# A decoder layer: the second MLP matrix as Strassen block products, with its running result and the sums of weight blocks in HBM

## Chip, cores and metric

The kernel runs on one core of a Trainium2 chip. The metric is the device time of one execution in microseconds (us). The kernel before takes 1024.85 us, the median of three runs (1024.71 to 1026.03).

## The reference

One decoder layer over 576 tokens: a prompt of 512 and 8 samples of 8 tokens. The width is 1024, the MLP is 4096 wide, all in 32-bit floats.

```
h = rmsnorm(x); z = h @ w_in                       # 1024 -> 6912
retention, window attention and short convolution  # "the mixer"
mixed = sum_n sigmoid(gate_n) * (branch_n @ w_branch_n) @ w_out
x = x + rmsnorm(mixed)
f = square(relu(rmsnorm(x) @ w_ff1)) @ w_ff2       # 1024 -> 4096 -> 1024
x = x + rmsnorm(f)
x = x + sigmoid(rmsnorm(x) @ w_ple_gate) * (p @ w_ple_proj)
```

## The kernel before

Activations lie feature by feature: 8 blocks of 128 features on the partitions, 576 tokens along a row, worked in two halves of 288. Every product is done with three matmuls, because both factors are split into a high part (rounded to the format that TensorE reads, `fp32r`) and a low part: high x high, high x low, low x high.

All weights lie in one tensor `W` of panels, in the order of use. A panel is 128 x 1024 (512 KB): mostly the 8 blocks that make one output column of 128 features. `prep` (L140 to L142) loads a panel on SP's queue into `wst` (2 buffers), ScalarE casts the high part `whi`, VectorE subtracts to get the low part `wlo` (3 buffers each); `nextw` prepares two panels ahead. `unit` (with `mm`, L324) does one panel: 8 blocks x 3 matmuls x 2 halves = 48 matmuls into two PSUM banks `pm`. `stats` and `rsqrt` make the norms: a matmul, VectorE, a power on GpSimd (L378), VectorE again.

The order on each engine is a scheduler's: it walks the instructions by priority and puts each on its engine's queue when its model has the inputs and a free buffer. An engine then works through its queue in order. SP only issues DMAs.

The program has the mixer (from the start to about 496 us), the output projection with the first norm, and the MLP in four quarters c of 1024 hidden features. A quarter is eight columns of the first matrix (f1) and then eight panels of the second (f2), whose result is added into a tile `f` in SBUF (L983). For c = 0, f1 and f2 are plain units. For c = 1 to 3, f1 is done in pairs of columns (m, m+4) by a Strassen (Winograd) scheme: the 8 x 2 blocks of a pair's weights and the two halves of the tokens make a 2 x 2 problem, with 7 block products of 12 matmuls in place of 8 (`pairs`, `product`, L216). The sums of operand blocks (`xs`) are made once, for the norm's output. The four sums of weight blocks of a pair, t3, t2, t1 and t4, are made on VectorE (`Pair.prep`, L182, L188, L192, L197) just before the split into high and low parts (L162, L163). After each product the `done_a` function takes relu and square (L1020 to L1029). f2 is plain units in every quarter.

At the end of the MLP stand `handover` (second norm and the start of the last gate) and eight gate panels with the output.

Of the kernel before, what the change touches and what calls it, by code (L numbers as in the profile page):

```python
# [1 line left out]

# [27 lines left out]
def panels():  # L30

    out = []
# [23 lines left out]
    out.append([("pp", k, m) for m in range(4) for k in range(2)])  # L56
    for c in range(4):
        if c == 0:
            cols("f1", range(8))
        else:  # L60
            for m in range(8 * c, 8 * c + 4):
                cols("f1", [m + 4, m])
        out.extend([[("f2", 8 * c + k, m) for k in range(8)] for m in range(8)])
    out.append([("pp", k, m) for m in range(4, 8) for k in range(2)])
    cols("pg", range(8))
    return out
# [3 lines left out]
def decoder_step(ctx: ExitStack, tc: tile.TileContext, xT, pT, W, consts, smalls, s0q, s0t, ckT, cv,  # L70
# [49 lines left out]
    plan = panels()  # L120
# [26 lines left out]
    def wtile():  # L147
        ph, pl = wpools[nprep[0] % len(wpools)]
        nprep[0] += 1
        return (ph.tile([P, 8, P], F32R, tag="whi", name=nm("whi")), pl.tile([P, 8, P], F32R, tag="wlo", name=nm("wlo")))  # L150
# [9 lines left out]
    def whalves(raw, n=8):  # L160
        hi, lo = wtile()
        A.copy(out=hi[:, :n, :], in_=raw[:, :n, :])  # L162
        V.tensor_tensor(out=lo[:, :n, :], in0=raw[:, :n, :], in1=hi[:, :n, :].bitcast(F32), op=ALU.subtract)  # L163
        return hi, lo
# [4 lines left out]
    class Pair:  # L169
# [7 lines left out]
        def prep(self, j):  # L177
            Q = 4 * P
            a, c = rawtile(), rawtile()
            load(c, W[j])  # L180
            load(a[:, :4, :], W[j + 1][:, :Q])
            V.tensor_tensor(out=a[:, 4:, :], in0=c[:, :4, :], in1=c[:, 4:, :], op=ALU.add)  # L182
            g = whalves(a)
            self.w["b11"], self.w["t3"] = (g, 0), (g, 4)
            yield
            b = rawtile()
            load(b[:, 4:, :], W[j + 1][:, Q:])
            V.tensor_tensor(out=b[:, :4, :], in0=a[:, :4, :], in1=a[:, 4:, :], op=ALU.add)  # L188
            g = whalves(b)
            self.w["t2"], self.w["b21"] = (g, 0), (g, 4)  # L190
            yield
            V.tensor_tensor(out=c[:, :4, :], in0=c[:, :4, :], in1=a[:, :4, :], op=ALU.add)  # L192
            g = whalves(c)
            self.w["t1"], self.w["b22"] = (g, 0), (g, 4)
            yield
            d = rawtile()
            V.tensor_tensor(out=d[:, :4, :], in0=b[:, :4, :], in1=b[:, 4:, :], op=ALU.add)  # L197
            self.w["t4"] = (whalves(d, 4), 0)
            yield
# [18 lines left out]

    class Operands:


        def __init__(self, xh, xl):
            self.xh, self.xl = xh, xl
            self.s = []

        def make(self, src, j):

            xa, xb = tmpt(), tmpt()
            src(j, xa)
            src(j + 4, xb)  # L230
            t = stmp.tile([P, 4, H], F32, tag="stmp", name=nm("stmp"))
            V.tensor_tensor(out=t[:, 0, :], in0=xb[:, HS[1]], in1=xa[:, HS[1]], op=ALU.subtract)
            V.tensor_tensor(out=t[:, 1, :], in0=xa[:, HS[0]], in1=t[:, 0, :], op=ALU.subtract)
            V.tensor_tensor(out=t[:, 2, :], in0=xa[:, HS[0]], in1=xa[:, HS[1]], op=ALU.add)
            V.tensor_tensor(out=t[:, 3, :], in0=xb[:, HS[0]], in1=t[:, 1, :], op=ALU.subtract)
# [3 lines left out]
            split(t, hi, lo)  # L239
            self.s.append((hi, lo))  # L240

        def __call__(self, name):
            if name in ("a11", "a12", "a22"):
                k0, h = 4 * (name[2] == "2"), HS[name[1] == "2"]
                return lambda j: (self.xh(k0 + j)[:, h], self.xl(k0 + j)[:, h])
            i = ("s1", "s2", "s3", "x3").index(name)
            return lambda j: (self.s[j][0][:, i, :], self.s[j][1][:, i, :])
# [4 lines left out]
    def pairs(js, X, make, done, ahead):  # L252
# [3 lines left out]
        prev = None  # L256
        for i, j in list(enumerate(js)) + [(None, None)]:
            q = None
            if i is not None:
                while len(groups) < i + 1 or "t1" not in groups[i].w:  # L260
                    next(make)
                q = Job()
                q.w, q.n = groups[i].w, i
                q.a, q.e, q.b = bank("pa"), bank("pe"), bank("pbb")
                product(q.a, q.w["b11"], X("a11"), True)
                A.activation(q.b[:, :H], q.a[:, :H], AF.Copy, scale=-1.0)
                product(q.e, q.w["t3"], X("s3"), True)
                q.es = halft()
                A.copy(out=q.es, in_=q.e[:, :H])
                next(make, None)  # L270
            if prev is not None:
                product(prev.e, prev.w["t4"], X("a22"), False)
                done(prev, "c21")
            if q is not None:
                product(q.b, q.w["t2"], X("s2"), False)
                A.copy(out=q.e[:, :H], in_=q.b[:, :H])
                next(make, None)
                product(q.a, q.w["b21"], X("a12"), False)
                done(q, "c11")
            if prev is not None:  # L280
                product(prev.b, prev.w["b22"], X("x3"), False)
                done(prev, "c12")
# [4 lines left out]
            elif ahead:  # L287
                ahead()
# [907 lines left out]
```

## Time and profile before

| | |
|---|---|
| median of three runs | 1024.85 us |
| the profiled execution | 1025.21 us |
| its span | 1023.4 us |
| TensorE busy, granted clock | 99%, 0.998 of full speed |
| VectorE, ScalarE, GpSimd busy | 59%, 37%, 5% |
| HBM read, written | 91.33 MB, 8.29 MB |

The span is the time from the first to the last instruction that the profiler saw; 1.8 us lie around it. Busy times count an engine's instructions once where they overlap. In the groups of instructions a mean is that of one instruction by itself; matmuls overlap, so means of theirs add up to more than the time that passed. A DMA share is the mean busy share of the core's 16 DMA engines.

### The profile page before, as it was taken

How to read it: one execution, taken by the hardware profiler on the slowest of the kernel's cores; microseconds unless marked ns; L12 is line 12 of the kernel's file. 1: busy time of each engine (PE TensorE's matmuls, PEld its weight loads, DVE VectorE, ACT ScalarE, POOL GpSimd, SP SyncE). 2: the span in 40 equal slices, each digit the busy share in tenths (PEclk: the TensorE clock that was granted, in tenths of full speed). 3: DMA queues.
4: the chain of work that ended last, by engine and by line, in shares of the span. 5: the costliest groups of instructions: out<-in, count | busy, mean ns of one | idle time of the engine just before them, and what ended most of it. 6: DMA issues, size and time to landing. Idle time of an engine off the chain costs nothing.

```text
span 1023.4 us, 17804 instructions
## 1 busy us (share of the span) xinstructions
PE 1009.6 (99%) x7477; PEld 977.8 (96%) x7477; DVE 603.0 (59%) x1119; ACT 383.5 (37%) x656; POOL 46.1 (5%) x49
## 2 busy tenths in 40 slices
PE   9999999999999999999999999999999999999998
PEld 8999999999999888899999999999999999999988
DVE  7534755543536766355528886267447744863886
ACT  7122322221213534233436544256225512653641
POOL 1100111000110000000001100000000000000110
PEclk9999999999999999999999999999999999999999
DMA  7321211222362211225413522123212511551122
GB/s 257 102 84 68 83 61 66 88 93 94 102 212 63 62 47 58 83 84 175 147 62 109 176 83 83 42 83 124 94 42 73 178 49 62 175 203 53 62 80 76
DMA packets 32112, 100.77 MB, mean 98 GB/s; under 512 B 3784, under 2 KB 6888, under 8 KB 31136
## 3 DMA queue, kind: packets, MB, share of 16 engines
q1 hardware_dynamic: 30672, 93.63, 28.3%
q0 software_dynamic: 1216, 5.94, 1.5%
q8 instruction: 58, 0.95, 0.4%
q14 instruction: 22, 0.18, 0.1%
q10 hardware_dynamic: 144, 0.06, 0.0%
HBM read 91.33 MB, written 8.29 MB: 97 GB/s over the span
## 4 chain that ended last, share of the span: by engine, by line
PE 84%; DVE 10%; DMA 2%; ACT 1%; issue 1%; POOL 1%; SPq 0%; POOLq 0%; DVEq 0%; ACTq 0%
PE pm L324 68%; PE pbb L216 4%; PE pa L216 3%; PE pe L216 3%; DMA wst<-in_W 1%; PE pb L732 1%; DVE wlo L142 1%; POOL rs_b L378 1%; DVE xl L402 1%; DVE hlf L907 1%; DVE x L908 1%; PE pb L713 1%; DVE fl L998 1%; PE pb L739 1%; DVE wlo L163 1%
## 5 line engine op out<-in xcount | busy, mean ns | idle before, releaser
L324 PE MATMUL pm<-xh,whi 128*128 128x288 f32 x1120 | 257.2, 301 | 0.8 <-ACT xh L401 0.4
L141 ACT CAST whi<-wst 128x1024 fp32r<-128x1024 f32 (+1 forms) x130 | 130.9, 1008 | 329.3 <-PE pm L324 253.9
L324 PE MATMUL pm<-xl,whi 128*128 128x288 f32 x1120 | 252.0, 296 | 2.1 <-DVE xl L402 2.0
L324 PE MATMUL pm<-xh,wlo 128*128 128x288 f32 x1120 | 251.6, 296 | 2.1 <-DVE wlo L142 2.1
L324 PEld LDWEIGHTS pm<-xh,whi 128*128 128x128 f32 x1120 | 183.7, 189 | 13.6 <-issue 8.4
L324 PEld LDWEIGHTS pm<-xl,whi 128*128 128x128 f32 x1120 | 183.8, 188 | 4.3 <-DVE xl L402 3.1
L324 PEld LDWEIGHTS pm<-xh,wlo 128*128 128x128 f32 x1120 | 183.9, 188 | 2.6 <-DVE wlo L142 2.6
L142 DVE TENSOR_TENSOR wlo<-wst,whi 128x1024 fp32r<-128x1024 f32 (+1 forms) x130 | 152.2, 1172 | 36.5 <-ACT whi L141 33.1
L324 PE MATMUL pm<-fl,whi 128*128 128x288 f32 x512 | 115.7, 298 | 1.9 <-DVE fl L998 1.9
L324 PE MATMUL pm<-fh,whi 128*128 128x288 f32 x512 | 115.9, 298 | 0.1
L324 PE MATMUL pm<-fh,wlo 128*128 128x288 f32 x512 | 115.5, 297 | 0.0
L410 DVE TENSOR_TENSOR tmp<-pm,rb 128x288 f32<-128x288 f32 x80 | 33.3, 451 | 97.2 <-PE pm L324 97.2
L324 PEld LDWEIGHTS pm<-fl,whi 128*128 128x128 f32 x512 | 84.6, 190 | 2.2 <-DVE fl L998 2.2
L324 PEld LDWEIGHTS pm<-fh,whi 128*128 128x128 f32 x512 | 84.6, 190 | 0.4 <-ACT fh L996 0.3
L324 PEld LDWEIGHTS pm<-fh,wlo 128*128 128x128 f32 x512 | 84.7, 190 | 0.0
L162 ACT CAST whi<-wst 128x1024 fp32r<-128x1024 f32 (+1 forms) x48 | 44.6, 942 | 95.3 <-PE pm L324 59.2
L378 POOL TENSOR_TENSOR rs_b<-rs_a,mhalf 128x9 f32<-128x9 f32 (+2 forms) x15 | 33.2, 2212 | 773.0 <-DVE rs_a L377 773.0
L163 DVE TENSOR_TENSOR wlo<-wst,whi 128x1024 fp32r<-128x1024 f32 (+1 forms) x48 | 51.8, 1089 | 26.7 <-ACT whi L162 25.1
L216 PE MATMUL pbb<-xs,whi 128*128 128x288 f32 x288 | 58.2, 295 | 0.0
L983 DVE TENSOR_TENSOR f<-f,pm 128x288 f32<-128x288 f32 x48 | 19.9, 450 | 47.9 <-PE pm L324 47.9
L216 PEld LDWEIGHTS pbb<-xs,whi 128*128 128x128 f32 x288 | 46.2, 188 | 0.0
L216 PE MATMUL pbb<-xs,wlo 128*128 128x288 f32 x144 | 42.5, 295 | 0.0
(248 smaller groups left out, 1478.4 us busy)
## 6 DMA issues: line engine op xcount, KB each, us to landing
wst<-in_W SPq DMA_DIRECT2D x134, 512.0 KB, 3.5
wst<-in_W SPq DMA_DIRECT2D x24, 256.0 KB, 2.6
x<-in_xT SPq DMA_DIRECT2D x10, 288.0 KB, 4.8
dx<-x POOLq DMA_DIRECT2D x2, 1152.0 KB, 4.6
x<-dx SPq DMA_DIRECT2D x2, 1152.0 KB, 7.2
out_yT<-x SPq DMA_DIRECT2D x16, 144.0 KB, 1.8
x<-in_xT SPq DMA_DIRECT2D x3, 576.0 KB, 6.6
tmp<-in_pT SPq DMA_DIRECT2D x4, 288.0 KB, 4.0
```

Source lines behind the costliest of these rows:

```text
L141: A.copy(out=hi[:, c, :], in_=st[:, c, :])
L142: V.tensor_tensor(out=lo[:, c, :], in0=st[:, c, :], in1=hi[:, c, :].bitcast(F32), op=ALU.subtract)
L162: A.copy(out=hi[:, :n, :], in_=raw[:, :n, :])
L163: V.tensor_tensor(out=lo[:, :n, :], in0=raw[:, :n, :], in1=hi[:, :n, :].bitcast(F32), op=ALU.subtract)
L216: PE.matmul(bank[:, :H], lhsT=lhs[:, s + j, :], rhs=rhs, start=start and j == 0 and i == 0, stop=j == 3 and i == 2, skip_group_check=True)
L324: PE.matmul(p[:, :H], lhsT=lhs[:, kw, :], rhs=rhs[:, HS[i]], start=s, stop=e)
L378: G.tensor_tensor(out=b, in0=a, in1=mhalf[:, :nb], op=ALU.pow)
L402: V.scalar_tensor_tensor(lo, src, gain(gi, k), hi.bitcast(F32), op0=ALU.mult, op1=ALU.subtract)
L410: V.tensor_tensor(out=out[:, HS[i]], in0=ps[i][:, :H], in1=r[:, HS[i]], op=ALU.mult)
L713: PE.matmul(p[g][:, i * w:i * w + w], lhsT=aq[grow(g), t + i, 128 * n:128 * n + 128], rhs=ak[grow(g), k0:k0 + w], start=True, stop=True)
L732: PE.matmul(po[grow(g), :], lhsT=avt[:, 128 * chunk + 64 * g:128 * chunk + 64 * g + 64], rhs=sb, start=kh == 0, stop=kh == nk - 1)
L983: V.tensor_tensor(out=fm, in0=fm, in1=ps[i][:, :H], op=ALU.add)
```

## The change

For c = 1 and 2 all eight columns of f2, and for c = 3 four of them, are done as pairs by the same scheme: pairs (m, m+4), for c = 3 (m, m+2). The square of the relu is stored in four quarter tiles `fq`, high and low halves together, and `Operands.make` builds the operand sums for f2 from the relu's results inside f1's pairs. Products of the last pair of f1 are finished by `rest` in front of f2's first pair, and that pair takes its products in another order.

The running result of f2 is no longer in SBUF. For c = 0 it is stored to eight HBM tensors `df` by SP; for c = 1 and 2 GpSimd adds to them by accumulating DMAs; for c = 3 they are loaded into `f`.

The four weight sums of all 22 pairs (12 of f1, 10 of f2) are built in HBM. A generator, `weight_sums`, has six stretches (five of 4 pairs, one of 2), two at a time, each in six steps; `nextw` calls for one step. A full stretch has DMAs of 1 MB: plain copies on SP, accumulating ones on GpSimd. `Pair.prep` then only loads pieces and splits them. The pools for split weights are smaller (one extra buffer for two, and two half buffers for t4).

```diff
+    def weight_sums():
+        def steps(j0, n):
+            t3, t2, t1, t4 = [spill.tile([P, n, Q], F32, name=nm("ts")) for _ in range(4)]
...
+            for t in (t3, t1):
+                nc.sync.dma_start(out=t, in_=block(0, 0))
+            yield
+            G.dma_start(out=t3, in_=block(0, 1), accum_op=ALU.add)
+            G.dma_start(out=t1, in_=block(1, 0), accum_op=ALU.add)
+            yield
+            nc.sync.dma_start(out=t2, in_=t3)
+            yield
+            G.dma_start(out=t2, in_=block(1, 0), accum_op=ALU.add)
+            yield
+            nc.sync.dma_start(out=t4, in_=t2)
+            yield
+            G.dma_start(out=t4, in_=block(1, 1), accum_op=ALU.add)
+            yield
+        for a in range(0, len(stretches), 2):
+            gens = [steps(*q) for q in stretches[a:a + 2]]
+            for _ in range(6):
+                for g in gens:
+                    next(g)
+                    yield
...
     def nextw(ahead=2):
+        next(wsums, None)
         j = pos[0]
...
-            V.tensor_tensor(out=a[:, 4:, :], in0=c[:, :4, :], in1=c[:, 4:, :], op=ALU.add)
-            g = whalves(a)
...
+            t3, t2, t1, t4 = sums[j]
+            for parts in ((("b11", W[j + 1][:, :Q]), ("t3", t3)), (("t2", t2), ("b21", W[j + 1][:, Q:])),
+                          (("t1", t1), ("b22", W[j][:, Q:])), (("t4", t4),)):
+                n = 4 * len(parts)
+                raw = rawtile()
+                hi, lo = wtile(n)
+                for i, (name, src) in enumerate(parts):
+                    load(raw[:, 4 * i:4 * i + 4, :], src)
+                    self.w[name] = (hi, lo), 4 * i
+                A.copy(out=hi, in_=raw[:, :n, :])
+                V.tensor_tensor(out=lo, in0=raw[:, :n, :], in1=hi.bitcast(F32), op=ALU.subtract)
+                yield
...
+    def rest():
+        q = last.pop()
+        product(q.b, q.w["b22"], q.X("x3"), False)
+        q.done(q, "c12")
+        product(q.e, q.w["t4"], q.X("a22"), False)
+        q.done(q, "c21")
...
+    def done_f(c, n):
+        def done(q, which):
...
+            if which in ("c21", "c12"):
+                G.dma_start(out=df[m], in_=q.t[m2], accum_op=ALU.add)
...
+    for c in range(1, 4):
+        Fc = Quads()
+        F[:] = [Fc, ((1, 0),) if c < 3 else (), Operands(Fc.at)]
+        pairs(4, ops, done_a)
+        n = 4 if c < 3 else 2
+        fops = F[2]
+        if c == 3:
+            rest()
+            f, X1, pps[0] = Act8(F32, "f"), Act8(F32, "x1"), bigt(F32, "pp")
+            for k in range(8):
+                nc.sync.dma_start(out=f(k), in_=df[k])
...
+        pairs(n, fops, done_f(c, n), True)
+    rest()
```

In what follows, `wst` are panels on their way in, `cst` the constants, `ts` the HBM tensors of the sums (of the first stretch: ts30 is t3, ts31 t2, ts32 t1, ts33 t4; of the second: ts58, ts59, ts60, ts61). SP's queue near the start, before:

```order
L449 DMA cst_112<-in_consts 128x2118
L140 DMA wst30_304<-in_W 128x1024
L140 DMA wst33_310<-in_W 128x1024
L140 DMA wst54_406<-in_W 128x1024
L140 DMA wst59_464<-in_W 128x1024
L140 DMA wst64_522<-in_W 128x1024
L140 DMA wst69_580<-in_W 128x1024
```

And of the change, from the same place (units 3 to 8 of the weights):

```order
L187 DMA ts30_304<-in_W 512x1x512
L187 DMA ts32_306<-in_W 512x1x512
L149 DMA wst34_310<-in_W 128x1024
L149 DMA wst37_316<-in_W 128x1024
L517 DMA cst_112<-in_consts 128x2118
L187 DMA ts58_412<-in_W 512x1x512
L187 DMA ts60_414<-in_W 512x1x512
L149 DMA wst62_418<-in_W 128x1024
L149 DMA wst67_478<-in_W 128x1024
L192 DMA ts31_305<-ts30_304 16x16384
L192 DMA ts59_413<-ts58_412 16x16384
L149 DMA wst72_538<-in_W 128x1024
```

Four copies of 1 MB have come ahead of the weights of unit 5, and two copies that need finished accumulates ahead of those of unit 7. Later on SP's queue, units 17 to 21 before:

```order
L140 DMA wst141_1177<-in_W 128x1024
L140 DMA wst156_1259<-in_W 128x1024
L140 DMA wst169_1349<-in_W 128x1024
L140 DMA wst176_1420<-in_W 128x1024
L140 DMA wst186_1492<-in_W 128x1024
```

And of the change, units 17 to 20 (ts280 to ts283 belong to the fifth stretch, ts295 to ts298 to the sixth):

```order
L149 DMA wst157_1213<-in_W 128x1024
L187 DMA ts295_2174<-in_W 256x1x512
L187 DMA ts297_2176<-in_W 256x1x512
L192 DMA ts281_2071<-ts280_2070 16x16384
L149 DMA wst172_1297<-in_W 128x1024
L192 DMA ts296_2175<-ts295_2174 16x8192
L149 DMA wst185_1389<-in_W 128x1024
L196 DMA ts283_2073<-ts281_2071 16x16384
L196 DMA ts298_2177<-ts296_2175 16x8192
L149 DMA wst192_1461<-in_W 128x1024
```

The last of all 24 copies stands directly ahead of the weights of unit 20; after it SP's queue holds no copy of sums any more. GpSimd's queue near the start, before (`rs_b` is the power of the first norm's two halves):

```order
L461 MEMSET rq50_395 128x2304
L378 ISA
L378 TENSOR_TENSOR rs_b41_347<-rs_a40_346,mhalf_94 128x9
L378 TENSOR_TENSOR rs_b47_385<-rs_a46_384,mhalf_94 128x9
L640 COPY co_948<-ubuf122_1027 128x2
```

And of the change (a DMA here is an accumulating one):

```order
L529 MEMSET rq54_401 128x2304
L189 DMA ts30_304<-in_W 512x1x512
L190 DMA ts32_306<-in_W 512x1x512
L446 ISA
L446 TENSOR_TENSOR rs_b45_353<-rs_a44_352,mhalf_94 128x9
L189 DMA ts58_412<-in_W 512x1x512
L446 TENSOR_TENSOR rs_b51_391<-rs_a50_390,mhalf_94 128x9
L190 DMA ts60_414<-in_W 512x1x512
L194 DMA ts31_305<-in_W 512x1x512
```

Two accumulates have come ahead of the first half's power and a third between the halves.

## Rows read from the trace of the kernel before

**Rows 1.** The page: span, then busy us, share and count of each engine.
```profile
span 1023.4 us, 17804 instructions
PE 1009.6 (99%) x7477; PEld 977.8 (96%) x7477; DVE 603.0 (59%) x1119; ACT 383.5 (37%) x656; POOL 46.1 (5%) x49
```
**Rows 2.** The page: the chain that ended last, by engine and by line.
```profile
PE 84%; DVE 10%; DMA 2%; ACT 1%; issue 1%; POOL 1%; SPq 0%; POOLq 0%; DVEq 0%; ACTq 0%
PE pm L324 68%; PE pbb L216 4%; PE pa L216 3%; PE pe L216 3%; DMA wst<-in_W 1%; PE pb L732 1%; DVE wlo L142 1%; POOL rs_b L378 1%; DVE xl L402 1%; DVE hlf L907 1%; DVE x L908 1%; PE pb L713 1%; DVE fl L998 1%; PE pb L739 1%; DVE wlo L163 1%
```
**Rows 3.** TensorE's waits, longest first: us in total, times, longest.
```profile
PE pm L324 <- DVE wlo L142: 2.1, 2, 1.3
PE pm L324 <- DVE xl L402: 2.0, 2, 1.2
PE pm L324 <- DVE fl L998: 1.9, 1, 1.9
```
**Rows 4.** Groups of f2's matmuls: busy us, mean ns of one, idle before.
```profile
L324 PE MATMUL pm<-fl,whi 128*128 128x288 f32 x512 | 115.7, 298 | 1.9 <-DVE fl L998 1.9
L324 PE MATMUL pm<-fh,whi 128*128 128x288 f32 x512 | 115.9, 298 | 0.1
L324 PE MATMUL pm<-fh,wlo 128*128 128x288 f32 x512 | 115.5, 297 | 0.0
```
**Rows 5.** Stretches: length, busy us (count) by engine, clock, DMA share, GB/s.
```profile
5.00:16.00 11.00, 10.54 (x71) 9.37 (x70) 9.62 (x17) 10.16 (x21) 1.53 (x1) 1.00 1.00 373
420.00:470.00 50.00, 50.00 (x376) 50.00 (x377) 24.03 (x37) 14.15 (x18) 0.00 (x0) 1.00 0.28 88
667.00:935.00 268.00, 267.39 (x2003) 266.42 (x2002) 167.36 (x255) 117.38 (x174) 0.00 (x0) 1.00 0.34 109
```
**Rows 6.** Groups on VectorE: one of four block additions, weight splits.
```profile
L142 DVE TENSOR_TENSOR wlo<-wst,whi 128x1024 fp32r<-128x1024 f32 (+1 forms) x130 | 152.2, 1172 | 36.5 <-ACT whi L141 33.1
L163 DVE TENSOR_TENSOR wlo<-wst,whi 128x1024 fp32r<-128x1024 f32 (+1 forms) x48 | 51.8, 1089 | 26.7 <-ACT whi L162 25.1 <-PE pe L216 1.1
L182 DVE TENSOR_TENSOR wst<-wst 128x512 f32<-128x512 f32 x12 | 8.3, 690 | 19.0 <-DMA wst<-in_W 18.9
```
**Rows 7.** Groups on VectorE: 288 and 576 wide.
```profile
L908 DVE TENSOR_TENSOR x<-x,hlf 128x288 f32<-128x288 f32 x32 | 13.8, 450 | 0.0
L1029 DVE TENSOR_TENSOR fl<-tmp,fh 128x576 fp32r<-128x576 f32 x24 | 17.9, 755 | 3.8 <-ACT tmp L1028 3.8
```
**Rows 8.** GpSimd in order of time: start us, us, what [idle before].
```profile
25.42 1.80 POOL L378 TENSOR_TENSOR rs_b<-rs_a,mhalf 128x9 f32<-128x9 f32 x1 [18.89 <-DVE rs_a L377]
29.87 1.80 POOL L378 TENSOR_TENSOR rs_b<-rs_a,mhalf 128x9 f32<-128x9 f32 x1 [2.65 <-DVE rs_a L377]
```
**Rows 9.** ScalarE in order of time: casts of units 20, 21 and 22.
```profile
130.36 1.05 ACT L141 CAST whi<-wst 128x1024 fp32r<-128x1024 f32 x1 [2.33 <-PE pm L324]
...
137.56 1.05 ACT L141 CAST whi<-wst 128x1024 fp32r<-128x1024 f32 x1 [3.52 <-PE pm L324]
144.80 1.05 ACT L141 CAST whi<-wst 128x1024 fp32r<-128x1024 f32 x1 [6.18 <-PE pm L324]
```
**Rows 10.** SP's issues in order of time.
```profile
9.58 0.39 SPq L449 DMA_DIRECT2D cst<-in_consts  x1
```
**Rows 11.** DMA issues: count, KB each, us to landing.
```profile
wst<-in_W SPq DMA_DIRECT2D x134, 512.0 KB, 3.5
...
dx<-x POOLq DMA_DIRECT2D x2, 1152.0 KB, 4.6
x<-dx SPq DMA_DIRECT2D x2, 1152.0 KB, 7.2
```

More of the change, by code (lines that the diff above doesn't have):

```diff
@@ L1 @@
 from contextlib import ExitStack
+from itertools import chain
 import concourse.bass as bass
@@ L158, in rawtile, with block @@
         return pool.tile([P, 8, P], F32, tag="wst", name=nm("wst"))
[L160 to L164, printed above, removed]
+    Q = 4 * P
+    sums = {}
+    def weight_sums():
+        def steps(j0, n):
+            t3, t2, t1, t4 = [spill.tile([P, n, Q], F32, name=nm("ts")) for _ in range(4)]
+            for i in range(n):
+                sums[j0 + 2 * i] = [t[:, i, :] for t in (t3, t2, t1, t4)]
+            def block(first, half):
+                return W[j0 + first:j0 + 2 * n:2, :, Q * half:Q * half + Q].rearrange("j p q -> p j q")
+            for t in (t3, t1):
[18 more added lines that the diff above has]
+                    yield
     def load(dst, src):
@@ L250, in decoder_step @@
         pass
[L252 to L270, printed above, removed]
-            if prev is not None:
[L272 to L277, printed above, removed]
+    made = [0]
@@ new lines, in decoder_step, with weights, pairs @@
+    last = []
+    def weights():
+        while len(groups) <= made[0] or "t2" not in groups[made[0]].w:
+            next(make)
+        made[0] += 1
+        return groups[made[0] - 1].w
+    def rest():
[4 more added lines that the diff above has]
+        q.done(q, "c21")
+    def pairs(n, X, done, own=False):
+        for i in range(n):
+            if own and i == 0 and last:
+                rest()
+            prev = last.pop() if last else None
+            q = Job()
+            q.w, q.n, q.X, q.done = weights(), i, X, done
+            q.a, q.b = bank("pa"), bank("pbb")
+            product(q.a, q.w["b11"], X("a11"), True)
+            A.activation(q.b[:, :H], q.a[:, :H], AF.Copy, scale=-1.0)
+            if own and i == 0:
+                product(q.a, q.w["b21"], X("a12"), False)
+                done(q, "c11")
+            q.e = bank("pe")
+            product(q.e, q.w["t3"], X("s3"), True)
+            q.es = halft()
+            A.copy(out=q.es, in_=q.e[:, :H])
+            next(make, None)
+            if prev is not None:
+                product(prev.e, prev.w["t4"], prev.X("a22"), False)
+                prev.done(prev, "c21")
+            product(q.b, q.w["t2"], X("s2"), False)
+            A.copy(out=q.e[:, :H], in_=q.b[:, :H])
+            next(make, None)
+            if not (own and i == 0):
@@ L280, in pairs @@
             if prev is not None:
-                product(prev.b, prev.w["b22"], X("x3"), False)
-                done(prev, "c12")
-            if q is not None:
-                product(q.b, q.w["t1"], X("s1"), False)
-                done(q, "c22")
-                next(make, None)
-            elif ahead:
-                ahead()
-            prev = q
+                product(prev.b, prev.w["b22"], prev.X("x3"), False)
+                prev.done(prev, "c12")
+            next(make, None)
+            product(q.b, q.w["t1"], X("s1"), False)
+            done(q, "c22")
+            next(make, None)
+            last.append(q)
     def need(j):
@@ L1010, in done_a, with halves @@
+    def halves(t):
+        return [t[:, h] for h in HS]
     def done_a(q, which):
         m, i = q.n + 4 * (which[2] == "2"), int(which[1]) - 1
[L1013 to L1023 removed]
@@ new lines, in gained @@
+    def gained(k):
+        t = tmpt()
+        A.activation(t, X1(k), AF.Copy, scale=gain(2, k))
+        return halves(t)
+    F = [Quads(), (), None]
+    made_pairs = [j0 + 2 * i for j0, n in stretches for i in range(n)]
+    make = chain(prep_pairs(made_pairs), prep(made_pairs[-1] + 2), prep(made_pairs[-1] + 3))
+    XH, XL, rb = handover(MH, ML, evac_mix, mix, 2, "2", evac_a)
+    G.dma_start(out=dpp, in_=pps[0])
+    ops = Operands(lambda i, k: (XH(k)[:, HS[i]], XL(k)[:, HS[i]]))
+    for m in range(SKEW + 1, 8):
+        evac_a(m, unit(nextw(), XH, XL, ident_k, ident_k), rb)
+        ops.make(gained(m - SKEW - 1), gained(m - 1))
@@ L1149 @@
     }
[L1150 removed]
+    plan, _ = panels()
     W = np.empty((len(plan), P, 8, P), np.float32)
```

255 lines of the change are left out of this document (139 added, 116 removed).

## Prediction

> **What bounds the kernel now.** I read the page's busy times first [rows 1]: TensorE is busy 99% of the span, VectorE 59%, ScalarE 37%, GpSimd 5%. The chain that ended last says the same: 84% of it is TensorE, 68% one line, the general unit L324 [rows 2]. The table of waits then shows that TensorE hardly waits: no releaser costs it more than 2.1 us over the whole run [rows 3]. So a matmul less is time less, and a wait that TensorE does not have today is time more, one for one.
>
> The price of a matmul is not the mean in the groups. They show some 298 ns [rows 4], but successive matmuls overlap; the stretch from 420 to 470 us, with no idle time, holds 376 of them in 50.00 us [rows 5], which is 133 ns each.
>
> **What the change removes.** The second MLP matrix takes 3 x 512 = 1536 matmuls [rows 4], 384 for each quarter c. With seven block products for eight, c = 1 and c = 2 lose 48 each; c = 3, where two of four column pairs are done so, loses 24. 120 x 133 ns = 16.0 us off TensorE. All of it is on the path. The four block additions per pair of the first matrix (12 pairs at 0.69 us each, [rows 6]) leave VectorE: 33 us, worth nothing by themselves, as VectorE has room.
>
> **What it adds on VectorE and ScalarE in the MLP.** Ten new pairs need 3.5 weight splits in place of 2: 15 x 1.09 us = 16 us on VectorE. Operand sums for the second matrix are made 12 times: four 288-wide operations at 0.45 us [rows 7], a 288-wide split at 0.45 and an 864-wide one at 1.02 (an estimate between the 576-wide 0.755 us and the 1024-wide 1.17 us [rows 6, 7]): 3.3 us, in all 39 us. The low halves now come in halves (+2 us), the additions into the sum in SBUF become partly DMA (-5 us). Net 19 us on VectorE in the stretch from 667 to 935 us, where it is busy 167 of 268 us [rows 5]: 186 of about 252, so throughput is not the limit. The accumulating DMAs of the running result (16 of 288 KB) and the reload of it (2.4 MB) lie in a stretch with a DMA share of 0.34; I cost them at nothing. TensorE's next 22 us of pairs hide the reload; without that cover it is 2.36 MB at the rate below, 6 us.
>
> The exception is latency where the first matrix of a quarter hands over to the second. The last block of the first is an operand of the second. From its last product to the low half of the third operand the bare chain is subtraction, relu, square, four sums and two splits, 5.5 us. On VectorE stand 18 instructions there: 13 of 0.45 us, two 864-wide at 1.02, three weight splits of 0.69 to 1.17 [rows 6, 7], 10.4 us. TensorE has 69 matmuls to do meanwhile, 9.2 us. That leaves a wait of 0 to 4 us at each of the three handovers; I take 1.5, nearest to the sum: +4.5 us.
>
> **What it adds in the mixer.** This is the large term. The sums of all 22 pairs are built in HBM: four sums of 256 KB per pair, each by one plain copy on SP's queue and one accumulating DMA on GpSimd's. 22 x 4 x 0.262 MB = 23.07 MB of copies and as much of accumulates. The source issues one step per weight unit, but the order on SP is denser: all 24 copies stand ahead of the weights of unit 20 (units counted from 0 in the order of W; the rows of SP's queue stand with the change). SP takes its instructions in order, and four of six steps wait: the copy t2 <- t3 for the accumulate into t3, the copy t4 <- t2 for that into t2. Queued behind each such copy are the weights of the next units; for them wait ScalarE's cast, VectorE's low half and TensorE. On GpSimd the accumulates wait for the copies, and behind them stand the power operations of the norms; today the first two run at 25.42 and 29.87 us [rows 8], the second now stands behind an accumulate whose copy is issued after the constants, and VectorE holds the next weight split behind it.
>
> How much time is there? Today the weights of unit 20 are cast at 130.36 us, and TensorE reaches that unit at 144.80, where the cast of unit 22 gets the buffer that unit 19 frees [rows 9]. Less cast and split (1.05 + 1.17 us) they must land by 142.6. The first copy can go at 9.58 us, where the constants are issued today [rows 10]. That is 133 us.
>
> How much traffic goes before them? The 23.07 MB of copies; the accumulates without the last two, 21.5 MB; 18 weight loads and the constants, 10.5 MB. The rate is in the trace: from 5 to 16 us the 16 DMA engines have a share of 1.00 and move 373 GB/s [rows 5]. That is loads from HBM to SBUF. No row shows a transfer from HBM to HBM or an accumulate, so both are bounded. Below: each byte counts once, 55.1 MB / 373 = 148 us, 15 us too long. Above: reading and writing each cost a pass, a copy two, an accumulate (two operands read, one written) three: 123.7 + 172.9 + 28.2 = 325 us, 192 us too long. I take one pass per operand read, since the 373 is a rate of reading with the write beside it: 61.8 + 115.3 + 28.2 = 205 us, 72 us too long. A lower bound of zero holds only if rate and overlap are better than the saturated row.
>
> The Trainium skill, Collectives: The Full Stack, section on the bandwidth ceiling, says that an add in the DMA path halves the rate because it reads two sources over one ring; no run here shows it yet. It is the rule that speaks against this change, and by it the accumulates cost two passes.
>
> The power operations and the queue's own waits lie inside these 72 us: while data move, it does not matter who waits for whom. A gap after a wait can also bring the granted clock down; after such gaps the traffic still sets the pace, so I add nothing.
>
> **Sum.** Profiled execution 1025.2 us (span 1023.4 and 1.8 around it), 0.4 above the median of the three runs: 1025.2 - 16.0 + 4.5 + 72 - 0.4 = 1085.
>
> **Rivals.**
> *HBM to HBM is dearer than reading.* If the writes share the engines' time with the reads, the excess is 192 us and the time 1205; halfway it is about 1145. For it: single loads of 1152 KB back from HBM take 7.2 us and stores 4.6 [rows 11], so neither side is free. Against: the loads at 373 GB/s write as they read.
> The Trainium skill, DMA: Bandwidth & Descriptors, section Latency and other measured facts, gives 207 to 214 GB/s in each direction for copies between HBM tensors. By an estimate from that page, copies and accumulates at 210 take 212 us, with the loads 240, and the time would be 1120; no row here shows such a copy.
>
> *The traffic hides.* If an accumulate costs no more than a copy and the long rows of these copies (64 KB for t2 and t4) move faster than the loads, the excess goes to nothing: 1025.2 - 16.0 + 4.5 - 0.4 = 1013, faster. The point from which it decides is an excess of 11.5 us, which is 16.0 less 4.5: 55.1 MB in 144.5 us, 381 GB/s. For it: the present share between 420 and 470 us is only 0.28 [rows 5]. Against: 44.6 MB over 17 units are 2.6 MB more for a unit that takes some 7 us [rows 9], which alone is 375 GB/s, beside its own weights.
>
> *The change does not do what it says.* The traffic hides, but the handovers cost their upper bound of 4 us each and the buffers for split weights, four in place of five, add as much: the 16 us go, and the time is 1025. For it: VectorE's queue there is longer than TensorE's cover. Against: 0.34 DMA share and 62% VectorE in that stretch [rows 5].
>
> **Chances and range.** Forecast (excess 40 to 110 us, own range 1050 to 1125) 0.54; dearer HBM traffic 0.25; hidden 0.16; no gain 0.05. The predicted time is the first: 1085. Leaving out part of the hidden case and the far end of the dear one, 2 in 10 together, the range is 1018 to 1180; the unknown price of an accumulate makes it so wide. A difference under 0.2% (2 us) can't be told from none: faster 0.16, same 0.05, slower 0.79.
>
> **What the next profile would show.** Right: a DMA share near 1.0 from about 20 to 215 us and normal after it; TensorE idle some 70 us there, in gaps that end with a weight split, behind SP waits for the tensors ts; landing times of weights far above today's 3.5 us [rows 11]; 120 matmuls fewer; waits of 1 to 2 us at three places after 700 us. Wrong: TensorE dense before 215 us, a share that stays under 0.8, or the gaps standing in the MLP.

## The result and the profile after

The changed kernel takes 1174.67 us, the median of four runs (1171.16 to 1178.0), against 1025.16 us for the kernel before on the same chip: 1.146 times as long (95% interval 1.142 to 1.150). I forecast 1085, slower by 6%; it is slower by 14.6%. The direction was right. The time lies near the end of the range (1018 to 1180), and outside the 1050 to 1125 that I gave the forecast itself: the size was wrong.

The page of the profiled execution, its first lines [rows 1]:

```profile
span 1171.1 us, 18120 instructions
PE 1020.1 (87%) x7357; PEld 979.2 (84%) x7357; DVE 614.3 (52%) x1161; ACT 434.9 (37%) x809; POOL 88.4 (8%) x89
```

TensorE has the 120 matmuls fewer, but it is busy 87% of the span in place of 99%. Its row of the 40 slices (tenths busy, 29 us each) says where, and the row of the DMA engines stands beside it:

```profile
PE   9496732219999999999999999999999999988998
DMA  9899778895123362121243225244567658656222
```

The holes are in slices 2 to 9, up to 263 us, where the DMA engines are at 70% or more. After that TensorE is dense. In the chain by lines [rows 2] the general unit has 45% in place of 68%, and DMAs have come in: 4% for `wst<-ts`, 3% for `wst<-in_W`, 2% for `ts<-in_W`.

TensorE's longest waits [rows 3] were 2.1 us each before; now they are:

```profile
PE pm L392 <- ACT whi L150: 52.0, 6, 20.1
PE pm L392 <- DVE bgt L560: 36.5, 1, 36.5
```

The cast of `whi` waits for weights to land, and 36.5 us stand behind one VectorE instruction, `bgt` L560. It comes at the end of a norm's chain, and in that chain VectorE waits 39.7 us for one power on GpSimd. The stretches of [rows 5], with the place of the sums (20 to 260) and the part from the output projection on (columns: length, busy us (count) of PE, PEld, DVE, ACT, POOL, then clock, DMA share, GB/s):

```profile
20.00:260.00 240.00, 117.55 (x777) 113.87 (x776) 48.33 (x84) 23.54 (x31) 31.77 (x28) 0.74 0.88 215
633.90:1171.10 537.20, 510.02 (x3690) 498.20 (x3688) 350.91 (x656) 284.63 (x547) 31.76 (x27) 0.99 0.49 147
```

From 5 to 16 us nothing has changed: 372 GB/s at a share of 1.01. From 20 to 260 TensorE does 777 matmuls, where the kernel before does 1819, at a granted clock of 0.74, and the DMA engines move only 215 GB/s at a share of 0.88. So the engines were mostly busy, yet slow per byte.

How much the mixer lost can be read from ScalarE's casts. The pattern of idle times of [rows 9] (2.33, 3.52, 6.18 us, each ended by TensorE) comes back; the last two rows here are units 21 and 22:

```profile
267.82 1.05 ACT L150 CAST whi<-wst 128x1024 fp32r<-128x1024 f32 x1 [1.34 <-PE pm L392]
...
275.04 1.05 ACT L150 CAST whi<-wst 128x1024 fp32r<-128x1024 f32 x1 [3.53 <-PE pm L392]
282.27 1.05 ACT L150 CAST whi<-wst 128x1024 fp32r<-128x1024 f32 x1 [6.18 <-PE pm L392]
```

Unit 21 is cast at 275.04 us, before at 137.56: 137.5 us late. The first product with `mh`, where the output projection begins, is late by the same 137.5 us (633.9 against 496.4), so nothing is lost or regained between. From there to the end the change takes 537.2 us, before 527.0: 10.2 us more, where I had 11.5 less.

GpSimd in order of time [rows 8]; a DMA here is an accumulating one:

```profile
33.45 1.19 POOL L190 DMA_DIRECT2D ts<-in_W  x1 [14.23 <-issue]
34.20 2.41 POOL L446 TENSOR_TENSOR rs_b<-rs_a,mhalf 128x9 f32<-128x9 f32 x1
48.06 1.22 POOL L189 DMA_DIRECT2D ts<-in_W  x1 [11.45 <-issue]
48.77 2.37 POOL L446 TENSOR_TENSOR rs_b<-rs_a,mhalf 128x9 f32<-128x9 f32 x1
...
138.28 1.18 POOL L190 DMA_DIRECT2D ts<-in_W  x1 [8.47 <-issue]
147.65 1.16 POOL L189 DMA_DIRECT2D ts<-in_W  x1 [8.19 <-issue]
156.64 1.18 POOL L190 DMA_DIRECT2D ts<-in_W  x1 [7.83 <-issue]
```

The two powers have moved from 25.42 and 29.87 us to 34.20 and 48.77, each straight behind an accumulate. Up to 224 us the accumulates start 9 to 17 us apart, and what precedes nearly all of them is "issue": no semaphore that the profile shows holds GpSimd up. At 138 to 157 us, with several inputs ready, they come every 9 us. SP's issues [rows 10] near the start:

```profile
17.68 0.42 SPq L517 DMA_DIRECT2D cst<-in_consts  x1
...
33.21 24.73 SPq L192 DMA_DIRECT2D ts<-ts  x2
```

and at the end of the sums:

```profile
257.11 3.02 SPq L196 DMA_DIRECT2D ts<-ts  x2
260.35 34.88 SPq L149 DMA_DIRECT2D wst<-in_W  x6
```

The constants are issued at 17.68 us and not at 9.58; copies and the weights behind them wait until 58 us. The last two copies go at 257 to 260, and the weights of unit 20 at 260.35. DMA issues to landing [rows 11]:

```profile
wst<-in_W SPq DMA_DIRECT2D x102, 512.0 KB, 3.5
wst<-ts SPq DMA_DIRECT2D x88, 256.0 KB, 3.6
ts<-in_W POOLq DMA_DIRECT2D x20, 1024.0 KB, 12.2
ts<-in_W SPq DMA_DIRECT2D x10, 1024.0 KB, 15.0
```

Weights by themselves still take 3.5 us as a median over the whole run; copies and accumulates of the sums, in the crowded mixer, take 15.0 and 12.2. Behind the mixer the splits of the pairs [rows 6] are 88 in place of 48, as dear each as I took them (1090 ns in the mean, before 1089).

### The profile page after: what moved, and what is told of

Read it like the earlier page. It is cut to its first block, busy times and chain, and to the rows that moved or that the text cites. A ratio compares the mean times of both kernels' runs of the same rounds, so it can differ in the third digit from the quotient of the medians.

```text
span 1171.1 us, 18120 instructions
## 1 busy us (share of the span) xinstructions
PE 1020.1 (87%) x7357; PEld 979.2 (84%) x7357; DVE 614.3 (52%) x1161; ACT 434.9 (37%) x809; POOL 88.4 (8%) x89
## 4 chain that ended last, share of the span: by engine, by line
PE 57%; issue 18%; DMA 10%; DVE 8%; ACT 4%; POOL 3%; SPq 1%; ACTq 0%; POOLq 0%; DVEq 0%
PE pm L392 45%; DMA wst<-ts 4%; DMA wst<-in_W 3%; PE pbb L248 3%; DVE wlo L230 3%; ACT whi L229 2%; PE pe L248 2%; PE pa L248 2%; DMA ts<-in_W 2%; PE pb L800 1%; POOL rs_b L446 1%; DVE xl L470 1%; PE pb L781 1%; DVE hlf L979 1%; DMA x<-in_xT 1%
## 5 line engine op out<-in xcount | busy, mean ns | idle before, releaser
L151 DVE TENSOR_TENSOR wlo<-wst,whi 128x1024 fp32r<-128x1024 f32 (+1 forms) x110 | 127.5, 1164 | 149.9 <-ACT whi L150 148.2
L230 DVE TENSOR_TENSOR wlo<-wst,whi 128x1024 fp32r<-128x1024 f32 (+1 forms) x88 | 95.6, 1090 | 87.1 <-ACT whi L229 86.7
L248 PE MATMUL pbb<-xs,whi 128*128 128x288 f32 x528 | 110.6, 301 | 5.5 <-ACT xs L473 2.5
L248 PEld LDWEIGHTS pbb<-xs,whi 128*128 128x128 f32 x528 | 85.7, 190 | 8.7 <-ACT pe L341 3.7
L248 PE MATMUL pbb<-xs,wlo 128*128 128x288 f32 x264 | 78.8, 298 | 0.3 <-DVE wlo L230 0.3
L392 PE MATMUL pm<-fq,whi 128*128 128x288 f32 x384 | 72.7, 303 | 3.3 <-ACT whi L150 3.3
L392 PEld LDWEIGHTS pm<-fq,whi 128*128 128x128 f32 x384 | 60.2, 194 | 3.6 <-ACT whi L150 3.5
L248 PEld LDWEIGHTS pbb<-xs,wlo 128*128 128x128 f32 x264 | 50.3, 190 | 0.7 <-DVE wlo L230 0.5
L392 PE MATMUL pm<-fq,wlo 128*128 128x288 f32 x192 | 47.6, 302 | 0.7 <-DVE wlo L151 0.7
L248 PE MATMUL pe<-xs,whi 128*128 128x288 f32 x176 | 37.1, 300 | 0.0
L248 PE MATMUL pa<-fq,whi 128*128 128x288 f32 x160 | 34.1, 300 | 2.7 <-ACT pbb L328 1.6
## 6 DMA issues: line engine op xcount, KB each, us to landing
ts<-in_W POOLq DMA_DIRECT2D x20, 1024.0 KB, 12.2
ts<-in_W SPq DMA_DIRECT2D x10, 1024.0 KB, 15.0
```

The lines of the kernel that those rows point to most:

```text
L151: V.tensor_tensor(out=lo[:, c, :], in0=st[:, c, :], in1=hi[:, c, :].bitcast(F32), op=ALU.subtract)
L230: V.tensor_tensor(out=lo, in0=raw[:, :n, :], in1=hi.bitcast(F32), op=ALU.subtract)
L248: PE.matmul(bank[:, :H], lhsT=lhs[:, s + j, :], rhs=rhs, start=start and j == 0 and i == 0, stop=j == 3 and i == 2, skip_group_check=True)
L392: PE.matmul(p[:, :H], lhsT=lhs[:, kw, :], rhs=r, start=s, stop=e)
```

## The experiments

I had three theories for the mixer: the engines pay for reads and writes alike (volume); the accumulates pass one at a time on GpSimd's queue and everything behind them waits (order); the weights come late because they share the engines. For the part behind it: the handovers, or the transfers that I had costed at nothing.

**The prices by themselves.** Two kernels that only move data, 1 MB a piece, differ in one number, the space for descriptors of GpSimd's queue.

```diff
-    nc = _bacc.Bacc("TRN2", ..., dynamic_dma_scratch_size=2048)
+    nc = _bacc.Bacc("TRN2", ..., dynamic_dma_scratch_size=16384)
```

Expected of the small one: 

> A kernel that computes nothing of the layer: it moves blocks of 1 MB, each stage walled off from the next, and measures the transfers that the trace of before did not show. Forecast's rates (one pass per operand read at 373 GB/s): a copy from HBM to HBM 2.8 us plus about 2 us of latency, an accumulate 5.6 us plus latency. Theory A (engines pay for reads and writes alike): copy 5.6, accumulate 8.4 us plus latency, and six in a row take six times that without the latency. Theory B (accumulates are let through one at a time on GpSimd's queue): one alone costs no more than under the forecast, but six independent ones start only as each former one drains, 8 to 9 us apart, with the DMA share far under 1.

Expected of the large one: 

> The same probe with eight times the space for descriptors of GpSimd's queue (16384 in place of 2048). Theory A: six accumulates take as long as with the small space, since the data set the pace. Theory B: GpSimd now issues them about 1.2 us apart and the six end sooner, by the latency of each, some 2 us x 5 or more.

With 2048, GpSimd's second and third of six independent accumulates:

```profile
78.79 1.18 POOL L118 DMA_DIRECT2D pa<-in_W  x1 [8.13 <-issue]
87.96 1.16 POOL L118 DMA_DIRECT2D pa<-in_W  x1 [7.99 <-issue]
```

and the stretches with six accumulates, with six copies within HBM of rows of 2 KB (as for t3 and t1), with six of rows of 64 KB (as for t2 and t4), and with eight loads to SBUF (length, POOL busy, clock, share, GB/s with each byte counted once):

```profile
69.50:124.00 54.50, 7.01 (x6) 1.00 0.72 115
46.70:69.00 22.30, 0.00 (x0) 1.00 0.90 282
175.50:196.00 20.50, 0.00 (x0) 1.00 0.91 307
219.00:232.00 13.00, 0.00 (x0) 1.00 0.83 323
```

With 16384, the six issues stand in one row, 7 us long, and the data follow at a share over 1:

```profile
68.04 7.05 POOL L118 DMA_DIRECT2D pa<-in_W  x6 [29.66 <-SPq L97]
```

```profile
68.00:102.00 34.00, 7.05 (x6) 1.00 1.04 185
```

The accumulate moves 185 GB/s when it streams: half of the loads' 373, as I had taken it (one pass per operand read). The Trainium skill, Collectives: The Full Stack, section on the bandwidth ceiling, says of a reduction between cores that the two reads of its add halve the rate; the trace of this accumulate within one core agrees. With the small space each waits for the one before, 9.2 us a piece at a share of 0.72, and 115 GB/s are left. A copy moves 282 or 307 GB/s, somewhat dearer than a load (323 here, 373 in the crowd of the start). The Trainium skill, DMA: Bandwidth & Descriptors, section Latency and other measured facts, gives 207 to 214 at best for copies in HBM, measured with rows 512 KiB and more apart; the copies here have other rows and are faster, and the measurement decides. So volume at read-and-write price (187 GB/s for a copy, 125 for an accumulate) is wrong, and one at a time is real.

**e3, the change with four times that space.**

```diff
-    bgt = mixer.enter_context(tc.tile_pool(name="bgt", bufs=5))
+    bgt = mixer.enter_context(tc.tile_pool(name="bgt", bufs=4))
...
-    xst = ctx.enter_context(tc.tile_pool(name="xst", bufs=1))
...
-    xtmp = ctx.enter_context(tc.tile_pool(name="xtmp", bufs=2))
+    xtmp = ctx.enter_context(tc.tile_pool(name="xtmp", bufs=1))
...
-    rawpools[:] = [wst, wst, xst]
+    rawpools[:] = [wst]
...
-    nc = _bacc.Bacc("TRN2", ..., dynamic_dma_scratch_size=2048)
+    nc = _bacc.Bacc("TRN2", ..., dynamic_dma_scratch_size=8192)
```

> The change with four times the space for descriptors of GpSimd's queue (8192 in place of 2048). To make room, bgt has 4 buffers for 5, xtmp 1 for 2, and the pool xst is gone, so only the mixer (start to the first product with mh, 633.9 us in the change, 496.4 before) is compared. By the probe, six accumulates of 1 MB then take 34 us in place of 56. If the mixer is long because accumulates pass one at a time: 22 MB of them at 5.4 us, 23 MB of copies at 3.5 us and 10.5 MB of loads at 2.8 us are 119 + 77 + 28 = 224 us in place of some 265, and the mixer gets 40 to 60 us shorter, 575 to 595. If the data volume sets the end whatever the order: 625 to 640.

The mixer ends at 582.4 us, 51.5 earlier than in the change, as the order theory said (575 to 595). The stretch with the sums and the casts of units 20 and 21:

```profile
20.00:205.00 185.00, 116.79 (x767) 112.62 (x765) 44.87 (x79) 22.08 (x27) 32.26 (x28) 0.82 1.08 276
```

```profile
215.99 1.05 ACT L150 CAST whi<-wst 128x1024 fp32r<-128x1024 f32 x1 [1.10 <-PE pm L392]
223.14 1.05 ACT L150 CAST whi<-wst 128x1024 fp32r<-128x1024 f32 x1 [3.47 <-PE pm L392]
```

Share 1.08 and 276 GB/s in place of 0.88 and 215. SP issues the weights of unit 20 at 208.75 us, and they are cast at 215.99, when TensorE frees a buffer: they landed no later than my forecast had them, 215. Yet unit 21 is 85.6 us late (223.14 against 137.56), not 72. (The whole takes 1156.2 us, 1.127 times before, interval 1.123 to 1.130: behind the mixer the given-up buffers stand against it, 570.4 us for 537.2 in the change.)

**e1 and e2, where the sums are not built in HBM.** e1 reads other weight blocks of the same size in the place of t3, t2, t1, t4; its output is not the layer's.

```diff
-        def steps(j0, n): ...
+        for j0, n in stretches:
+            for i in range(n):
+                j = j0 + 2 * i
+                sums[j] = [W[j][:, :Q], W[j + 1][:, :Q], W[j][:, :Q], W[j + 1][:, Q:]]
```

> The change without the traffic of the sums: t3, t2, t1 and t4 are read from plain weight blocks of the same size, so the output is not the layer's; the rest of the change stays. If the forecast's MLP terms hold (16.0 us of matmuls off, 4.5 us of handovers on): 1013 us. If the MLP loses what the trace of after seems to show (10.2 us longer than before from the first product of the output projection on): 1035 us, and then the sums cost about 137 us. If the MLP's loss comes from the mixer's state (clock, late queues): near 1013.

1026.5 us, ratio 1.0012 (1.0001 to 1.0022): the sums cost 148 us, and without them the pairs still gain nothing. From the output projection on:

```profile
496.50:1024.40 527.90, 506.45 (x3689) 496.61 (x3688) 350.28 (x656) 284.10 (x547) 31.68 (x27) 0.99 0.48 149
```

527.9 us against 527.0 before and 537.2 in the change.

e2 makes all sums on VectorE in SBUF with the `Pair.prep` of before.

> The change with the sums of weight blocks made on VectorE in SBUF as before, for all 22 pairs; pairs for the second matrix and the running result in HBM stay. If the MLP's loss lies in late weights (each pair loads 1 MB here in place of 1.75 MB): 1013 to 1020 us. If it lies in VectorE's and ScalarE's latency at the handovers: the 22 x 4 additions of 0.69 us make them later, 1035 to 1045 us. If in the accumulates of the running result: about 1030 us.

1049.9 us, 1.023 (1.022 to 1.025): slower than e1 by 23, above all of the outcomes that I had written. 88 additions of 0.69 us are 61 us of VectorE. The loss stands around the three handovers: from 700 to 740 us 233 matmuls for 282 in e1, from 800 to 840 225 for 287, from 900 to 960 298 for 375. That VectorE's queue is the reason is argued and not shown; the pieces of a pair also wait for each other longer here, and no run separates the two.

**e4, own queue, late.** Copies on GpSimd's queue too, stretch by stretch, each held back by a gate that reads a weight tile of units 6, 16, ... 56.

```diff
-            for t in (t3, t1):
-                nc.sync.dma_start(out=t, in_=block(0, 0))
+            g = sml.tile([P, 4], F32, tag="gate", name=nm("gate"))
+            A.copy(out=g, in_=wprep[pos[0]][0][:, 0, :4].bitcast(F32))
+            for t in (t3, t1):
+                G.dma_start(out=t[0:1, 0, :4], in_=g[0:1, :])
+                G.dma_start(out=t, in_=block(0, 0))
...
-            nc.sync.dma_start(out=t2, in_=t3)
+            G.dma_start(out=t2, in_=t3)
```

> The same sums by the same copies and accumulates, but the copies too on GpSimd's queue, one stretch after another, each stretch started by a small gate (a copy of four numbers of weight unit 6, 16, 26, 36, 46 or 56 to SBUF and from there into the tensor) so that it can't come earlier. SP's queue then holds no sums, and the traffic is spread over some 400 us. If the loss comes from the queue's order and from the traffic being crowded ahead of unit 20: 1026 to 1035 us, as without sums. If the traffic itself costs TensorE, by weights landing later, wherever it lies: over 1060. GpSimd's own operations (powers, small copies) wait for up to two accumulates, which could cost 0 to 30 us.

1089.5 us, 1.062 (1.060 to 1.065): by its number the second case (over 1060), but not by its reason. From 40 to 140 us the traffic runs beside a TensorE that never stops:

```profile
40.00:140.00 100.00, 100.00 (x761) 98.84 (x761) 48.09 (x81) 24.52 (x32) 16.29 (x21) 1.00 0.82 215
```

761 matmuls in 100 us at a DMA share of 0.82. But the mixer is 53.4 us longer than e1's, and TensorE's waits there, by the profile, end with VectorE instructions; the second fence has what VectorE itself waited for from 100 to 360 us (us in all, times, longest):

```profile
PE pb L668 <- DVE bgt L659: 19.3, 2, 10.5
PE pm L384 <- DVE tmp L470: 15.8, 1, 15.8
```

```profile
DVE rs_d L439 <- POOL rs_b L438: 43.1, 5, 21.0
DVE bgt L659 <- DMA out_o_rs<-bgt: 34.7, 2, 19.9
```

Powers and small stores of GpSimd, then, that stand behind accumulates in its queue. 43.9 us of TensorE's waits end with VectorE instructions (`bgt`, `tmp`) of these chains.

**e7, in the gaps.** The same with the stretches at units 6, 41, 49, 57 and the panels 0 and 4 of f2's quarter 0, where GpSimd has nothing else, and with the late reload of e5.

```diff
-        if j >= 6 and (j - 6) % 10 == 0:
+        if j in (6, 41, 49, 57, 83, 87):
```

> As e4, with the six stretches started at units 6, 41, 49 and 57 and at the first and fifth panel of the second matrix's quarter 0, where GpSimd has no power operations or copies of its own, and with the late reload of e5. If e4's remaining loss (its mixer is 53 us longer than e1's) is GpSimd's own operations waiting behind accumulates, as its 44 us of TensorE waits behind rs_b suggest, the mixer is within 5 us of e1's 496.5 and the time is 1030 to 1040 us. If the traffic itself costs there: 1060 or more.

1039.4 us, 1.014 (1.012 to 1.016), and the mixer is 496.8 us long, as without sums (496.5 in e1): both as expected. Two stretches:

```profile
300.00:400.00 100.00, 100.00 (x784) 88.69 (x783) 64.68 (x153) 40.58 (x109) 13.02 (x15) 1.00 0.83 213
660.00:720.00 60.00, 50.88 (x355) 50.18 (x355) 37.15 (x65) 31.61 (x60) 4.17 (x5) 0.92 0.75 202
```

At a share of 0.83 nothing is lost (300 to 400). At 660 to 720 the short stretch meets the loads of the first pairs, and 78 matmuls fewer are done than in e5. Beside the mixer's plain units, then, this traffic costs TensorE nothing; beside the MLP's pairs it does.

**e5 and e8, DMAs beside the pairs.** e5 is e1 with X1 and pp (the residual and the product `p @ w_ple_proj`, which the kernel before stores and reloads too) reloaded after the last pair; e8 is e5 with plain stores for the accumulating DMAs into `df` (the earlier quarters are lost).

```diff
 e5, in addition to e1
-            for k in range(2):
-                nc.sync.dma_start(out=X1.t[k], in_=dx[:, 4 * k:4 * k + 4, :])
-            nc.sync.dma_start(out=pps[0], in_=dpp)
         pairs(n, fops, done_f(c, n), True)
     rest()
+    for k in range(2):
+        nc.sync.dma_start(out=X1.t[k], in_=dx[:, 4 * k:4 * k + 4, :])
+    nc.sync.dma_start(out=pps[0], in_=dpp)
 e8, in addition to e5
-                G.dma_start(out=df[m], in_=q.t[m2], accum_op=ALU.add)
+                G.dma_start(out=df[m], in_=q.t[m2])
```

> As e1 (sums not built, output not the layer's), but the reload of X1 and pp (3.5 MB) comes after the last pair of the second matrix in the program, behind two weight panels on SP's queue. TensorE does 278 matmuls from 890 to 940 us in e1 where 388 would fit, 14 us lost. If the weights late behind the reload are the cause, 4 to 10 us come back: 1017 to 1022. If it is the handover's own chain (operand sums and splits): 1026 as e1.

> As e5 (1024.0 us; sums not built), and the 16 accumulating DMAs of the running result are plain stores, so the earlier quarters are lost from the result too. If accumulates (DMA share 0.8 to 0.9 beside the second matrix) are what delays the weights there: 1016 to 1020 us. If TensorE's losses are the handovers and splits alone: 1023 to 1025.

e5: 1024.0 us, 0.9985 (0.9974 to 0.9996), 2.5 less than e1, under what I had hoped. e8: 1015.6 us, 0.991 (0.989 to 0.993), 8.4 less than e5 (7.6 by the ratios; the two ran on different chips). The same stretch of f2's pairs of c = 1, first e5, then e8:

```profile
720.00:800.00 80.00, 78.22 (x580) 76.81 (x578) 48.57 (x77) 42.95 (x80) 6.89 (x8) 1.00 0.70 181
```

```profile
720.00:800.00 80.00, 79.75 (x598) 79.05 (x597) 52.95 (x85) 45.84 (x85) 4.38 (x8) 1.00 0.58 193
```

The share falls from 0.70 to 0.58 and TensorE does 598 matmuls for 580.

**e6, e9, e10, e11.** e6 is e2 with the additions on GpSimd (`G.tensor_tensor`).

> As e2 (1049.9 us, sums made in SBUF), but the 88 additions on GpSimd in place of VectorE. If VectorE's queue at the handovers made e2 23 us slower than e1: 1027 to 1035. If GpSimd takes more than 3 us for an addition or slows VectorE down, the weights come late: 1050 or more.

1076.3 us, 1.049 (1.047 to 1.051): worse, so GpSimd has no better place for them. An addition takes it 1.35 to 1.69 us, VectorE itself becomes slower (last section), and ScalarE's casts wait 42.9 us in all behind the additions for t4. e9 is e7 with the short stretch at unit 65, e10 is e9 with a load, an addition on VectorE and a store in place of each accumulate into `df`, and e11 is e9 with the sums laid pair by pair in HBM:

```diff
 e11
-            t3, t2, t1, t4 = [spill.tile([P, n, Q], F32, name=nm("ts")) for _ in range(4)]
+            t3, t2, t1, t4 = [spill.tile([n, P, Q + 16], F32, name=nm("ts"))[:, :, :Q].rearrange("j p q -> p j q")
+                              for _ in range(4)]
```

> As e7 (1039.4 us, its mixer as long as without sums), with the short stretch of the last quarter started at unit 65, so that it no longer meets the loads of the first pairs at 660 to 720 us, where e7 does 207 matmuls and e5 284 in 40 us, 10 us less. The full stretch of the last quarter but one starts at unit 83 as in e7. If that collision is what separates e7 from e5 (1024.0): 1024 to 1031 us. If the sums' tensors themselves load slower than the weights do (0.3 to 0.6 us later in the change than in e1): 1033 to 1038.

> As e9, and the 16 accumulating DMAs of the running result become a load of the earlier result to SBUF, an addition of 576 columns on VectorE (0.76 us) and a plain store, all its DMAs on GpSimd's queue. By e8 the accumulates cost 8.4 us beside the second matrix. If it is the accumulating itself (its share of the DMA engines): 5 to 8 us less than e9, 1017 to 1025, and faster than before in part of that range. If any second pass over the data costs as much, the same as e9; if the additions delay VectorE's weight splits, slower than e9.

> As e9 (1033.9 us), but the tensors ts lie pair by pair in HBM, rows of 2 KB 2112 bytes apart, where in e9 the rows of one pair lie 8 KB apart (for W the halves of a panel lie 4 KB apart). All instructions of TensorE, VectorE and ScalarE are in the same order. If the place of the rows in HBM makes the pieces ts land later than pieces of W, 4 to 9 us come back, 1025 to 1030. If not: the same as e9 within 2 us, and the 10 us between e9 and e5 are the sums' traffic itself.

e9: 1033.9 us, 1.0076 (1.0048 to 1.0105), the second case. e10: 1034.5 us, 1.0079 (1.0058 to 1.0100): no gain. That fits a second pass over the result, in whatever form, as what e8 was rid of, but the additions that e10 puts on VectorE could hide a gain, and no run separates the two. e11: 1026.0 us, 1.000 (0.998 to 1.002). TensorE, VectorE and ScalarE have the same instructions in the same order in e9 and e11; the median landings of 256 KB pieces, first e9, then e11:

```profile
wst<-ts SPq DMA_DIRECT2D x88, 256.0 KB, 3.7
wst<-in_W SPq DMA_DIRECT2D x66, 256.0 KB, 4.0
```

```profile
wst<-ts SPq DMA_DIRECT2D x88, 256.0 KB, 3.3
wst<-in_W SPq DMA_DIRECT2D x66, 256.0 KB, 3.5
```

By the median the pieces come 0.4 to 0.5 us earlier, and 8 us come back (3 to 12 by the two intervals). Only the place of the rows of `ts` differs. But the copies and accumulates that build the sums go to the other rows too, and the pieces of W, whose rows did not move, come earlier by as much; whether the loads of `ts` or the building of the sums gains first, and why, no run here tells. e11, which leaves nothing out, is as fast as the kernel before; of the kernels that leave nothing out none beat it.

## Why the prediction was off, step by step

**TensorE, 16.0 us.** Right: 120 matmuls fewer in every run, and e8 has most of the gain that this allows (9.4 us under before).

**Which resource, and where.** Right: the mixer, by the sums' traffic ahead of unit 20, with waits behind weight splits and powers.

**The rate, one pass per operand read.** Right for the accumulate when it streams (185 GB/s), 20 to 30% too good for the copy (307 and 282 in place of 373). The rival "dearer HBM" was wrong in its reason, though its numbers (1145 to 1205) hold the result.

**"While data move, it does not matter who waits for whom."** This is the step that failed. I had the in-order queues and put their waits inside the 72 us. But data do not always move: with the descriptor space of this kernel an accumulate of 1 MB drains before GpSimd issues the next. 24 accumulates (four of them of half the size) start from 17.88 to 265 us, 10.8 us apart; alone they take 9.2, streaming 5.7. e3, whose mixer differs in that space and in one `bgt` buffer fewer, gives 51.5 us back. The sign was in the list: "a share near 1.0"; it is 0.88 in the change and 1.08 in e3.

**The weights of unit 20 as the end of the loss.** Wrong as well. I let the loss end when those weights land, at 215 us, 72 us later than they may. The traces show another end. In the change TensorE's last long wait ends at 258.01 us, SP issues the weights of unit 20 only at 260.35, and from there to the output projection no wait of TensorE is longer than 0.2 us. The wait is the one for `bgt`, behind a norm's power on GpSimd: VectorE writes its input (`rs_a`) at 215.59 us, and GpSimd comes to it at 251.95, behind accumulates:

```profile
251.37 1.06 POOL L194 DMA_DIRECT2D ts<-in_W  x1 [5.22 <-DMA ts<-ts]
251.95 3.45 POOL L446 TENSOR_TENSOR rs_b<-rs_a,mhalf 128x16 f32<-128x16 f32 x1
258.01 0.88 PE L392 MATMUL pm<-xh,whi 128*128 128x288 f32 x2 [36.51 <-DVE bgt L560]
```

The same power before, and in e3:

```profile
112.46 2.90 POOL L378 TENSOR_TENSOR rs_b<-rs_a,mhalf 128x16 f32<-128x16 f32 x1 [6.57 <-DVE rs_a L377]
```

```profile
200.36 3.44 POOL L446 TENSOR_TENSOR rs_b<-rs_a,mhalf 128x16 f32<-128x16 f32 x1
```

It is 139.5 us late in the change and 87.9 in e3; the losses are 137.5 and 85.6. So the delay reaches TensorE through GpSimd's queue, and the 14.4 us between the cast of unit 20 (130.36) and TensorE's arrival, which I had counted as slack, do not help. The 13.6 us by which e3's loss exceeds my 72 are the difference between these two ends; no run prices them by themselves. That the fall of the clock adds little holds: behind the last wait the 18 matmuls from 258 to 262 us run at a granted clock of 0.55 and take some 1.6 us longer than 18 at 133 ns.

**"I cost them at nothing": accumulates and reload of the running result.** Wrong. A DMA share of 0.34 [rows 5] is a mean; where f2's pairs run it is 0.6 to 0.8 even without the sums (e5). e8 prices the accumulates at 8.4 us. The reload of the running result itself no run prices; the 2.5 us of e5 belong to the place of another reload, that of X1 and pp, for which the prediction has no term.

**Handovers, 4.5 us.** Too low. By the totals, what is left of e1 after those two is 1026.5 - 8.4 - 2.5 = 1015.6 against a forecast of 1013 for hidden traffic, 2.6 us more. By place, e8 does 131, 141 and 113 matmuls in the 20 us from 700, from 790 and from 890 us, where the kernel before does 153 from 700 to 720: some 3, 2 and 5 us, the third above the 4 that I had as the most. The third:

```profile
890.00:910.00 20.00, 17.01 (x113) 16.33 (x112) 13.49 (x25) 11.88 (x25) 0.00 (x0) 0.91 0.79 290
```

The smaller pools may have their share in it; no run has more buffers.

**The pieces of the sums land later than weights do.** Not in the prediction at all: the part from the output projection on is 537.2 us in the change and 527.9 in e1, and the pieces of 256 KB land in 3.6 us (`ts`) and 3.9 (W) there, in e1 in 3.3. That the place of the rows accounts for most of it is likely by e11, which was tried on e9 and not on the change itself.

The terms added up: 1025.2 - 16.0 + 4.5 + 72 + 13.6 + 51.5 + 8.4 + 2.5 + 9.3 + 2.6 = 1173.6, against 1174.7. That this fits so closely proves nothing: 72 + 13.6 + 51.5 is the loss of the mixer, divided at e3, and the other terms are differences between neighbouring runs from the change down to e8, so they must come near the total. The division rests on the runs, not on the sum.

## What to carry to other kernels

A saturated-bandwidth sum gives a bound and not a time: ask of each queue how many transfers it can have in flight, whether a wait in it leaves the engines idle, and what small instruction stands behind it; here the first was 52 of 148 us. Beside the mixer's units such traffic was free (share 0.83, nothing lost) where the weights had a queue of their own and the transfers started where their issuing engine had no other work. And a mean share does not show that a transfer is hidden: look at the stretch in which it runs.

## What was not expected of the hardware

Accumulating DMAs of 1 MB: 9.2 us apart with descriptor space 2048, 5.7 with 16384 (54.5 and 34 us for six). Copies within HBM at 282 and 307 GB/s. Pieces of 256 KB land in 3.7 us from rows 8 KB apart (e9) and in 3.3 us from rows 2112 bytes apart (e11). And GpSimd's additions slow VectorE: the group of subtractions `fq<-tmp,fq` in e1 and in e6:

```profile
L1056 DVE TENSOR_TENSOR fq<-tmp,fq 128x288 fp32r<-128x288 f32 x56 | 24.6, 452 | 4.1 <-ACT tmp L1055 4.0
```

```profile
L1071 DVE TENSOR_TENSOR fq<-tmp,fq 128x288 fp32r<-128x288 f32 x56 | 32.3, 595 | 4.3 <-ACT tmp L1070 4.2
```

The same 56 instructions take 595 ns in place of 452 (451 in e2, where VectorE does the additions), and an addition that takes VectorE 0.69 us takes GpSimd 1.35 to 1.69. The Trainium skill, SBUF — State Buffer, section SBUF: two separate sides, says that VectorE instructions with two operands in SBUF contend with GpSimd's reads; the trace agrees.
